# In the opening, TensorE sums the squares tile by tile and multiplies the first modulation tiles

## The chip, the cores and the metric

The kernel runs on one core of one Trainium2 chip, as one program with one launch. The metric is the device time in microseconds of one execution; times before are the median of three runs. A core has TensorE (PE; its weight loads are shown apart as PEld), VectorE (DVE), ScalarE (ACT), GpSimd (POOL) and SyncE (SP), each with its own queue in program order, and 16 DMA engines that carry the loads which SP issues.

## The reference, cut to what matters

Two transformer layers on 512 tokens of 1024 features, all in float32. The changed part is the very beginning of the first layer: the modulation vectors from `c`, the RMS norm of `x`, and the projection `h @ w_in` that reads it.

```python
c_act = jax.nn.silu(c)
for l in range(DEPTH):
    mod = c_act @ w_ada[l] + b_ada[l]
    sh1, sc1, g1, sh2, sc2, g2 = [t[:, None, :] for t in jnp.split(mod, N_ADA, axis=-1)]
    h = rmsnorm(x, norm_mix_g[l]) * (1.0 + sc1) + sh1
    z = h @ w_in[l]
    ...                                   # four attention mixers, then the gated output and the MLP
```

`rmsnorm` divides `x` by the root of the mean of its squares over the 1024 features and multiplies by a gain.

## The kernel before

Activations lie transposed: `x` is eight tiles `X["x"][k]` of 128 features by 512 tokens. A float32 product is made of three fp32r products: a weight tile is split into `whi` (ACT, line 87) and `wlo` (the rest, here on POOL in two halves, line 91), an activation tile into `hhi` and `hlo`, and PE multiplies hi by hi, hi by lo and lo by hi. `Weights` keeps the queue of weight tiles: `_load` issues the load into one of four raw buffers (line 72), `_split` makes hi and lo, and `get` runs ahead by `load_ahead` and `split_ahead`.

`start` is the opening. SP loads `x` (lines 165, 168), then two weight tiles, then the rest in the order of the code. PE first spreads the silu of `c` over all partitions (`cbP`, 8 products with the identity). ACT squares the eight tiles of `x`, DVE adds them up into `sqacc`, and PE turns the sum into four columns `nsum` with four one-column products (`ones` moves, the sum is the weight). DVE scales them (`rsv`, line 253), POOL takes the power -1/2 (`rs`, line 257), PE spreads the result over the partitions (`rsb`, line 263).

Then follows one turn for each tile k: `ada_start` loads two tiles of modulation weights (`ada`, 128 outputs by 1024, line 200), and DVE multiplies each by `cbP` and sums it into a column of `mod` (line 191); ACT makes the gain `gs`; DVE makes `ht = x * gs * rsb`; ACT adds the shift and rounds (`hhi`); ACT adds the shift again, and POOL subtracts for `hlo` (DVE does so from k = 5 on). Five weight tiles are fetched and split in the first turns, as `AHEAD` and `LAHEAD` say. Last come the 120 products `pj`: five weight tiles by eight k by three, with k outside.

A tile scheduler orders each engine's instructions from the order of the code and from marks like `tc.issue_after(last["ada"].ins)`, which put an instruction behind another in that order. An engine works its queue in order, so an instruction that waits holds up all that stand behind it.

Of the kernel before, what the change touches and what calls it, by code (L numbers as in the profile page):

```python
# [10 lines left out]
F32 = mybir.dt.float32  # L11
F32R = mybir.dt.float32r
AF = mybir.ActivationFunctionType
ALU = mybir.AluOpType
# [3 lines left out]
P = 128  # L18
S = 512
D = 1024  # L20
KT = D // P
NADA = 1
AHEAD = (1, 3, 2, 1, 0, 0)
LAHEAD = (2, 3, 2, 1, 0, 0)
PRELOAD = 2
NSPLIT = 3
# [5 lines left out]
NQ = S // P  # L32
# [6 lines left out]
OFF_NMIX, OFF_NMLP, OFF_BADA, OFF_QG, OFF_KVG, OFF_POS, OFF_SINK = 0, 8, 16, 64, 66, 67, 99  # L39
# [8 lines left out]
def wbytes_views(raw, k, n):  # L48
    return raw[:, 0 : k * n].rearrange("p (k n) -> p k n", k=k)


class Weights:
# [23 lines left out]
    def _split(self):  # L76
        i = self.n_split
        while self.n_load <= i:
            self._load()
        ap, k, n, split, rows, pool_lo = self.src[i]  # L80
        raw, flat = self.raws.pop(i)
        if split:
            pool, nb = self.other_pool.get(i, (self.hl_pool, None))
            hi = pool.tile([P, 1024], F32R, tag="whi", name=f"whi{i}", bufs=nb)
            lo = pool.tile([P, 1024], F32R, tag="wlo", name=f"wlo{i}", bufs=nb)
            vh, vl = wbytes_views(hi, k, n), wbytes_views(lo, k, n)
            self.nc.scalar.activation(vh[0:rows], raw[0:rows], AF.Copy)  # L87
            eng = self.nc.gpsimd if pool_lo else self.nc.vector
            for c in ((0, k * n // 2), (k * n // 2, k * n)) if pool_lo else ((0, k * n),):
                c = slice(*c)  # L90
                eng.tensor_tensor(  # L91
                    lo[0:rows, c], flat[0:rows, c], hi[0:rows, c].bitcast(F32), op=ALU.subtract
                )
            self.parts[i] = (vh, vl)
        else:
            self.parts[i] = (raw, None)
        self.n_split += 1
# [12 lines left out]
def layer_stack(ctx: ExitStack, tc: tile.TileContext, a, out):  # L110
    nc = tc.nc
# [5 lines left out]
    wkp = ctx.enter_context(tc.tile_pool(name="wkp", bufs=2))  # L117
    xp = ctx.enter_context(tc.tile_pool(name="xp", bufs=1))
    psA = ctx.enter_context(tc.tile_pool(name="psA", bufs=3, space=PSUM))
    psT = ctx.enter_context(tc.tile_pool(name="psT", bufs=2, space=PSUM))  # L120
# [3 lines left out]
    def mmbank(name):  # L124
        return psA.tile([P, 512], F32, tag="mm", name=name)
# [4 lines left out]
    vecs = cons.tile([P, NV], F32, name="vecs")  # L130
    nc.sync.dma_start(vecs, a["vecs"])
    X = {}
# [4 lines left out]
    ones = cons.tile([P, 1], F32, name="ones")  # L137
# [22 lines left out]
    def load_x(src, queue):  # L160

        v = xp.tile([P, KT // 2, S], F32, tag="V", name="x")
        tiles = [v[:, k, :] for k in range(KT // 2)]
        for k in (0, 2):
            queue.dma_start(v[:, k : k + 2, :], src[:, k : k + 2, :])
        for k in range(KT // 2, KT):
            tiles.append(xp.tile([P, S], F32, tag="KL", name="x", bufs=4))
            queue.dma_start(tiles[k], src[:, k, :])
        X["x"] = tiles


    cact = cons.tile([P, KT], F32, name="cact")
# [10 lines left out]
    mod = [cons.tile([P, 6, KT], F32, name=f"mod{l}") for l in range(DEPTH)]  # L183

    W = Weights(nc, rawp, hlp, 3, 3)
# [10 lines left out]
    def ada_start(pool, m, cv):  # L196

        raw = pool.tile([P, 2, 1024], F32, tag="ada0", name="ada0", bufs=4)
        for part in (1, 0):
            nc.sync.dma_start(raw[:, part, :], a["wadaP"][m, :, part, :])  # L200
            ada_cols(raw[:, part, :], 0, part, m, cv)
# [4 lines left out]
    last = {}  # L206
# [941 lines left out]
    def start(pool, n):  # L1148


        nonlocal psS
        load_x(a["xT"], nc.sync)
        for _ in range(PRELOAD):
            W._load()
        cps = ctx.enter_context(ExitStack())
        psC = cps.enter_context(tc.tile_pool(name="psC", bufs=1, space=PSUM))
        cbP = psC.tile([P, D], F32, name="cbP")
        for k in range(KT):
            nc.tensor.matmul(
                cbP[:, k * P : (k + 1) * P], cact[:, k : k + 1].to_broadcast([P, P]), ident,  # L1160
                start=True, stop=True,
            )
        acc = wkp.tile([P, S], F32, tag="sqacc", name="sqacc", bufs=1)
        nc.scalar.activation(acc, X["x"][0], AF.Square)
        for k in range(1, KT):
            sq = mmbank("sq")
            nc.scalar.activation(sq, X["x"][k], AF.Square)
            nc.vector.tensor_tensor(acc, acc, sq, op=ALU.add)
        rsb = psO.tile([P, 512], F32, tag="po", name="rsb0")
        ps = psT.tile([P, 512], F32, tag="pt", name="nsum")  # L1170
        for j in range(NQ):
            nc.tensor.matmul(
                ps[:, j : j + 1], acc[:, j * P : (j + 1) * P], ones, start=True, stop=True
            )
        r = rstd_cols(ps, NQ, [(0, NQ, 1.0 / D)])
        bcast_cols(rsb, r, 0, NQ)
        hs = h_tiles(hsp, "hs", 16)
        pss = [mmbank("pj") for _ in range(min(n, 3))]
        pss += [psT.tile([P, 512], F32, tag="pt", name="pj") for _ in range(min(n, 5) - 3)]
        W.other_pool.update({i: (pool, 4) for i in range(4)})  # L1180
        ws = []
        gs = smp.tile([P, KT], F32, tag="gs", name="gs")
        for k in range(KT):
            ada_start(pool, k, cbP)
            if k < n:
                W.split_ahead, W.load_ahead = AHEAD[k], LAHEAD[k]
                with tc.issue_after(last["pow"].ins):
                    ws.append(W.get())
            g = vecs[:, OFF_NMIX + k : OFF_NMIX + k + 1]
            nc.scalar.activation(  # L1190
                gs[:, k : k + 1], mod[0][:, 1, k : k + 1], AF.Identity, bias=g, scale=g
            )
            t = tmp_tile("ht")
            hi, lo = hs[k]
            with tc.issue_after(last["ada"].ins):
                last["dve"] = nc.vector.scalar_tensor_tensor(
                    t, X["x"][k], gs[:, k : k + 1], rsb, op0=ALU.mult, op1=ALU.mult
                )
            nc.scalar.activation(hi, t, AF.Identity, bias=mod[0][:, 0, k : k + 1])
            if k < KPOOL:  # L1200
                nc.scalar.activation(t, t, AF.Identity, bias=mod[0][:, 0, k : k + 1])
                nc.gpsimd.tensor_tensor(lo, t, hi.bitcast(F32), op=ALU.subtract)
            else:
                last["dve"] = nc.vector.scalar_tensor_tensor(
                    lo, t, mod[0][:, 0, k : k + 1], hi.bitcast(F32), op0=ALU.add, op1=ALU.subtract
                )
        for _ in range(NADA):
            i = ada_state["i"]
            raw = pool.tile([P, 2, 1024], F32, tag="ada0", name="ada0", bufs=4)
            nc.sync.dma_start(raw, a["wadaD"][i : i + 2].rearrange("t p r -> p t r"))  # L1210
            with tc.issue_after(last["dve"].ins):
                for j in range(2):
                    ada_cols(raw[:, j, :], *ada_todo[i + j], cbP)
            ada_state["i"] += 2
        W.split_ahead, W.load_ahead = 3, 3
        while W.n_split < n + NSPLIT:
            W._split()
        load_consts()
        nc.scalar.activation(cb, cbP, AF.Copy)
        cps.close()  # L1220
        psS = ctx.enter_context(tc.tile_pool(name="psS", bufs=2, space=PSUM))
        def part(g, w, k, h):
            nc.tensor.matmul(
                pss[g], ws[g][w][:, k, :], hs[k][h], start=(k + w + h == 0),
                stop=(k == KT - 1 and w == 1),
            )


        for k in range(KT - 1):
            for w, j, h in ((0, k, 0), (0, k - 1, 1), (1, k - 2, 0)):  # L1230
                if j >= 0:
                    for g in range(n):
                        part(g, w, j, h)
        k = KT - 1
        for g in range(n):
            for w, j, h in (
                (0, k - 1, 1), (1, k - 2, 0), (1, k - 1, 0), (0, k, 0), (0, k, 1), (1, k, 0)
            ):
                part(g, w, j, h)
        return hs, pss  # L1240
# [74 lines left out]
def _layout(i):  # L1315
    f = np.float32
    i = {k: np.asarray(v) for k, v in i.items()}
    a = _shape_constants()
# [6 lines left out]
    for l in range(DEPTH):  # L1325
        b = l * VL
# [13 lines left out]

    wa = i["w_ada"].transpose(0, 2, 1).reshape(DEPTH, 6, KT, P, D)
    a["wadaP"] = wa[0, 0:2].transpose(1, 2, 0, 3)
    a["wadaD"] = np.concatenate(
        [wa[0, j] for j in (2, 4, 3, 5)] + [wa[1, j] for j in (1, 0, 2, 4, 3, 5)]
    )
# [47 lines left out]
```

## Time and profile before

| | us |
|---|---|
| median of 3 runs | 1293.07 (1290.05 to 1298.04) |
| the profiled execution | 1297.35 |
| its span | 1295.4 |
| PE busy | 1242.8 (96%) |
| PE weight loads busy | 1046.6 (81%) |
| DVE busy | 691.1 (53%) |
| ACT busy | 592.1 (46%) |
| POOL busy | 541.3 (42%) |
| mean granted clock of PE | 0.98 |

Durations below come from the profiled execution, whose own time lies 4.3 us over the median. Busy shares are means over the whole span; in the first 32 us PE has 17.5 us of work, in most later stretches nearly all.

### The profile page before, as it was taken

To read this page: it belongs to the slowest core of one execution; us is meant where nothing else is said; L and a number is where in the kernel's file an instruction comes from. 1 tells how busy PE (TensorE), PEld (TensorE's weight loads), DVE (VectorE), ACT (ScalarE), POOL (GpSimd) and SP (SyncE) were. 2 spreads that over 40 slices of the span, in tenths; PEclk is the share of its full clock that TensorE was granted. 3 is DMA by queue.
4 is the path that set the end of the run, shared out by engine and by line. 5 is a ranking of instruction groups with operands and counts; after the bars stand their busy time and mean duration, and the time that the engine had idled before them with its cause. 6 is when DMAs were issued, how large, how long until landed. Compare 5 with 4: busy or idle time off the path is not lost. (4 is left out here: it accounts for less than half of the span.)

```text
span 1295.4 us, 18013 instructions
## 1 busy us (share of the span) xinstructions
PE 1242.8 (96%) x6572; PEld 1046.6 (81%) x6572; DVE 691.1 (53%) x1562; ACT 592.1 (46%) x1161; POOL 541.3 (42%) x463
## 2 busy tenths in 40 slices
PE   5989999988999999999999999999999999999997
PEld 4878787778888888888898777878988888888887
DVE  5758867966455454554254686786543213123124
ACT  5567768743532232231235766787353223233120
POOL 5423323242645545545425323323364444444440
PEclk7989999998999999999998999999999999999998
DMA  9744324353356766665434412122233323233312
GB/s 341 253 109 159 100 80 147 131 176 117 115 167 207 241 195 217 226 193 195 138 112 120 138 49 66 51 89 78 95 114 97 92 95 94 95 98 98 98 33 66
DMA packets 53129, 171.07 MB, mean 132 GB/s; under 512 B 6065, under 2 KB 9777, under 8 KB 53041
## 3 DMA queue, kind: packets, MB, share of 16 engines
q1 hardware_dynamic: 51312, 165.73, 40.0%
q10 hardware_dynamic: 1728, 4.20, 1.0%
q8 instruction: 52, 0.85, 0.3%
q14 instruction: 37, 0.30, 0.1%
HBM read 163.35 MB, written 4.19 MB: 129 GB/s over the span
## 5 line engine op out<-in xcount | busy, mean ns | idle before, releaser
L91 POOL TENSOR_TENSOR wlo<-raw,whi 128x512 fp32r<-128x512 f32 (+3 forms) x372 | 487.0, 1333 | 549.9 <-ACT whi L87 516.0
L87 ACT ACTIVATE whi<-raw 128x1024 fp32r<-128x1024 f32 (+3 forms) x186 | 193.8, 1046 | 452.8 <-PE px L368 244.5
L369 PE MATMUL pj<-hhi,wlo 128*128 128x512 f32 (+1 forms) x768 | 286.2, 373 | 0.0
L368 PE MATMUL pj<-hlo,whi 128*128 128x512 f32 (+1 forms) x768 | 285.7, 373 | 0.0
L367 PE MATMUL pj<-hhi,whi 128*128 128x512 f32 (+1 forms) x768 | 285.7, 374 | 0.0
L367 PE MATMUL px<-a,whi 128*128 128x512 f32 (+2 forms) x584 | 215.2, 368 | 0.0
L369 PE MATMUL px<-a,wlo 128*128 128x512 f32 (+2 forms) x584 | 214.5, 367 | 0.0
L368 PE MATMUL px<-a,whi 128*128 128x512 f32 (+2 forms) x584 | 213.7, 366 | 0.0
L411 DVE SCALAR_TENSOR_TENSOR x<-px,mod,x 128x512 f32<-128x512 f32 (+2 forms) x95 | 62.7, 665 | 195.1 <-PE px L369 195.0
L368 PEld LDWEIGHTS pj<-hlo,whi 128*128 128x128 f32 x768 | 144.9, 189 | 24.8
L369 PEld LDWEIGHTS pj<-hhi,wlo 128*128 128x128 f32 x768 | 144.9, 189 | 24.4
L367 PEld LDWEIGHTS pj<-hhi,whi 128*128 128x128 f32 x768 | 144.3, 189 | 22.9
L191 DVE CUSTOM_DVE_ANT_0 adaw<-cb,adaw,vecs 128x1024 f32<-128x1024 f32 x78 | 102.6, 1316 | 56.0 <-DMA adaw<-in_wadaD 54.0
L369 PEld LDWEIGHTS px<-a,wlo 128*128 128x128 f32 x584 | 109.8, 188 | 19.2
L368 PEld LDWEIGHTS px<-a,whi 128*128 128x128 f32 x584 | 109.8, 188 | 18.8
L367 PEld LDWEIGHTS px<-a,whi 128*128 128x128 f32 x584 | 109.9, 188 | 17.9
L1134 DVE SCALAR_TENSOR_TENSOR t<-pj,r 128x512 f32<-128x512 f32 x64 | 44.1, 692 | 141.4 <-ACT r L1133 141.2
L449 DVE TENSOR_TENSOR a<-t,a 128x512 fp32r<-128x512 f32 x64 | 82.8, 1296 | 41.8 <-ACT a L448 41.8
L592 ACT ACTIVATE e<-e,nm 128x256 f32<-128x256 f32 (+3 forms) x160 | 85.9, 538 | 10.1 <-DVE nm L587 9.8
L449 DVE TENSOR_TENSOR pl<-pt,ph 128x512 fp32r<-128x512 f32 (+1 forms) x112 | 65.5, 598 | 4.6 <-ACT ph L448 3.7
L626 PE MATMUL pt<-ident,e 128*128 128x128 f32 x376 | 61.0, 278 | 5.4 <-POOL e L570 4.9
L448 ACT ACTIVATE ph<-pt 128x512 fp32r<-128x512 f32 (+1 forms) x112 | 56.1, 524 | 17.7 <-PE pt L626 16.9
(236 smaller groups left out, 1829.9 us busy)
## 6 DMA issues: line engine op xcount, KB each, us to landing
adaw<-in_wadaD SPq DMA_DIRECT2D x78, 512.0 KB, 4.4
raw<-in_wup SPq DMA_DIRECT2D x64, 512.0 KB, 3.5
raw<-in_wdown SPq DMA_DIRECT2D x64, 512.0 KB, 3.6
raw<-in_winT SPq DMA_DIRECT2D x28, 512.0 KB, 3.7
ada<-in_wadaP SPq DMA_DIRECT2D x16, 512.0 KB, 8.9
raw<-in_wout SPq DMA_DIRECT2D x16, 512.0 KB, 3.6
cw<-in_cw SPq DMA_DIRECT2D x4, 512.0 KB, 5.1
raw<-in_cw SPq DMA_DIRECT2D x4, 512.0 KB, 4.6
```

The costliest lines, as they stand in the source:

```text
L87: self.nc.scalar.activation(vh[0:rows], raw[0:rows], AF.Copy)
L91: eng.tensor_tensor(lo[0:rows, c], flat[0:rows, c], hi[0:rows, c].bitcast(F32), op=ALU.subtract)
L191: last["ada"] = nc.vector.tensor_tensor_reduce(out=w, in0=cv, in1=w, scale=1.0, scalar=vecs[:, off : off + 1], op0=ALU.mult, op1=ALU.add, ...
L367: nc.tensor.matmul(ps, wh[:, k, :], hh[:, c], start=first, stop=False)
L368: nc.tensor.matmul(ps, wh[:, k, :], hl[:, c], start=False, stop=False)
L369: nc.tensor.matmul(ps, wl[:, k, :], hh[:, c], start=False, stop=last)
L411: last["dve"] = nc.vector.scalar_tensor_tensor(X["x"][m][:, c], ps, mod[l][:, part, m : m + 1], X["x"][m][:, c], op0=ALU.mult, op1=ALU.add)
L448: nc.scalar.activation(hi, src, AF.Copy)
L449: last["dve"] = nc.vector.tensor_tensor(lo, src, hi.bitcast(F32), op=ALU.subtract)
L592: nc.scalar.activation(e, e, AF.Exp, bias=nm[:, n : n + 1], scale=-1.0, accum_out=den[:, n : n + 1])
L626: nc.tensor.transpose(pt[:, c : c + P], p[n][:, col : col + P], ident)
L1134: nc.vector.scalar_tensor_tensor(t, ps, 0.0, r, op0=ALU.max, op1=ALU.mult)
```

## The change

The sums of squares are no longer added up on DVE. Each squared tile lies in SBUF (`tmp_tile`, four buffers) and PE multiplies it by `ones` at once, four one-column products a tile, summed in PSUM. The modulation tiles of k = 0 come in another layout (`wadaK`: 128 inputs by 8 by 128 outputs), are loaded right after `x` and ahead of the first two weights, and PE multiplies them by `cact` instead of DVE by `cbP`: eight one-column products for each of the two, the gain's (part 1) first, with ACT adding the bias into `mod`. DVE's `ada_start` begins with k = 1. The first split of a weight stands later (`AHEAD[0]` is 0), the first `hhi` is put behind the first `whi`, and one more split is asked for right after it.

```diff
--- before.py
+++ after.py
@@ -20,7 +20,7 @@
 D = 1024
 KT = D // P
 NADA = 1
-AHEAD = (1, 3, 2, 1, 0, 0)
+AHEAD = (0, 3, 2, 1, 0, 0)
 LAHEAD = (2, 3, 2, 1, 0, 0)
 PRELOAD = 2
 NSPLIT = 3
@@ -84,7 +84,7 @@
             hi = pool.tile([P, 1024], F32R, tag="whi", name=f"whi{i}", bufs=nb)
             lo = pool.tile([P, 1024], F32R, tag="wlo", name=f"wlo{i}", bufs=nb)
             vh, vl = wbytes_views(hi, k, n), wbytes_views(lo, k, n)
-            self.nc.scalar.activation(vh[0:rows], raw[0:rows], AF.Copy)
+            self.whi = self.nc.scalar.activation(vh[0:rows], raw[0:rows], AF.Copy)
             eng = self.nc.gpsimd if pool_lo else self.nc.vector
             for c in ((0, k * n // 2), (k * n // 2, k * n)) if pool_lo else ((0, k * n),):
                 c = slice(*c)
@@ -1150,6 +1150,9 @@
 
         nonlocal psS
         load_x(a["xT"], nc.sync)
+        first = pool.tile([P, 2, KT, P], F32, tag="ada0", name="ada0", bufs=4)
+        for part in (1, 0):
+            nc.sync.dma_start(first[:, part], a["wadaK"][part])
         for _ in range(PRELOAD):
             W._load()
         cps = ctx.enter_context(ExitStack())
@@ -1160,17 +1163,27 @@
                 cbP[:, k * P : (k + 1) * P], cact[:, k : k + 1].to_broadcast([P, P]), ident,
                 start=True, stop=True,
             )
-        acc = wkp.tile([P, S], F32, tag="sqacc", name="sqacc", bufs=1)
-        nc.scalar.activation(acc, X["x"][0], AF.Square)
-        for k in range(1, KT):
-            sq = mmbank("sq")
-            nc.scalar.activation(sq, X["x"][k], AF.Square)
-            nc.vector.tensor_tensor(acc, acc, sq, op=ALU.add)
         rsb = psO.tile([P, 512], F32, tag="po", name="rsb0")
         ps = psT.tile([P, 512], F32, tag="pt", name="nsum")
-        for j in range(NQ):
-            nc.tensor.matmul(
-                ps[:, j : j + 1], acc[:, j * P : (j + 1) * P], ones, start=True, stop=True
+        for k in range(KT):
+            sq = tmp_tile("sq")
+            nc.scalar.activation(sq, X["x"][k], AF.Square)
+            for j in range(NQ):
+                nc.tensor.matmul(
+                    ps[:, j : j + 1], sq[:, j * P : (j + 1) * P], ones,
+                    start=(k + j == 0), stop=(k == KT - 1 and j == NQ - 1),
+                )
+
+        aps = psT.tile([P, 512], F32, tag="pt", name="adap")
+        for part in (1, 0):
+            for k in range(KT):
+                nc.tensor.matmul(
+                    aps[:, part : part + 1], first[:, part, k, :], cact[:, k : k + 1],
+                    start=(k == 0), stop=(k == KT - 1),
+                )
+            b = OFF_BADA + 8 * part
+            nc.scalar.activation(
+                mod[0][:, part, 0:1], aps[:, part : part + 1], AF.Identity, bias=vecs[:, b : b + 1]
             )
         r = rstd_cols(ps, NQ, [(0, NQ, 1.0 / D)])
         bcast_cols(rsb, r, 0, NQ)
@@ -1181,7 +1194,8 @@
         ws = []
         gs = smp.tile([P, KT], F32, tag="gs", name="gs")
         for k in range(KT):
-            ada_start(pool, k, cbP)
+            if k:
+                ada_start(pool, k, cbP)
             if k < n:
                 W.split_ahead, W.load_ahead = AHEAD[k], LAHEAD[k]
                 with tc.issue_after(last["pow"].ins):
@@ -1192,12 +1206,16 @@
             )
             t = tmp_tile("ht")
             hi, lo = hs[k]
-            with tc.issue_after(last["ada"].ins):
+            with tc.issue_after(last["ada" if k else "pow"].ins):
                 last["dve"] = nc.vector.scalar_tensor_tensor(
                     t, X["x"][k], gs[:, k : k + 1], rsb, op0=ALU.mult, op1=ALU.mult
                 )
-            nc.scalar.activation(hi, t, AF.Identity, bias=mod[0][:, 0, k : k + 1])
+            with tc.issue_after(W.whi.ins if k == 0 else last["dve"].ins):
+                nc.scalar.activation(hi, t, AF.Identity, bias=mod[0][:, 0, k : k + 1])
+            if k == 0:
+                W._split()
             if k < KPOOL:
+              with tc.issue_after(W.whi.ins if k == 0 else last["dve"].ins):
                 nc.scalar.activation(t, t, AF.Identity, bias=mod[0][:, 0, k : k + 1])
                 nc.gpsimd.tensor_tensor(lo, t, hi.bitcast(F32), op=ALU.subtract)
             else:
@@ -1340,6 +1358,7 @@
 
     wa = i["w_ada"].transpose(0, 2, 1).reshape(DEPTH, 6, KT, P, D)
     a["wadaP"] = wa[0, 0:2].transpose(1, 2, 0, 3)
+    a["wadaK"] = np.stack([i["w_ada"][0][:, D * j : D * j + P].reshape(KT, P, P).transpose(1, 0, 2) for j in (0, 1)])
     a["wadaD"] = np.concatenate(
         [wa[0, j] for j in (2, 4, 3, 5)] + [wa[1, j] for j in (1, 0, 2, 4, 3, 5)]
     )
```

How the instructions stand on PE, from the start of the program to the first two `pj`, before (`cbP` is the spread of `c`, `rsb` that of the norm):

```order
L1159 MATMUL cbP<-ident,cact 128x128 x8
L1172 MATMUL nsum<-ones,sqacc 128x1 x4
L263 MATMUL rsb_170<-ident,rs 128x128 x4
L1223 MATMUL pj<-hhi,whi_213 128x512
L1223 MATMUL pj<-hhi,whi_218 128x512
```

and after:

```order
L1162 MATMUL cbP<-ident,cact 128x128 x8
L1172 MATMUL nsum<-ones,sq 128x1 x32
L1180 MATMUL adap<-cact,ada_131 128x1 x8
L263 MATMUL rsb_150<-ident,rs 128x128 x4
L1180 MATMUL adap<-cact,ada_131 128x1 x8
L1241 MATMUL pj<-hhi,whi_251 128x512
L1241 MATMUL pj<-hhi,whi_260 128x512
```

There are 28 more products of `nsum` and 16 of `adap` ahead of the first `pj`, and the spread of the norm stands between the two groups of `adap`.

On ACT, from the squares to the third weight's `whi`, before (`whi_213` and `whi_218` are the first two weights):

```order
L1164 ACTIVATE sqacc<-x 128x512
L1167 ACTIVATE sq<-x 128x512 x7
L87 ACTIVATE whi_213<-raw_131 128x1024
L87 ACTIVATE whi_218<-raw_133 128x1024
L1190 ACTIVATE gs<-mod_112,vecs 128x1
L87 ACTIVATE whi_238<-raw_211 128x1024
L1199 ACTIVATE hhi<-ht,mod_112 128x512
```

and after (`whi_251`, `whi_260` and `whi_276` are the first three):

```order
L1170 ACTIVATE sq<-x 128x512 x8
L1185 ACTIVATE mod_112<-adap,vecs 128x1
L1204 ACTIVATE gs<-mod_112,vecs 128x1
L1185 ACTIVATE mod_112<-adap,vecs 128x1
L87 ACTIVATE whi_251<-raw_134 128x1024
L1214 ACTIVATE hhi<-ht,mod_112 128x512
L87 ACTIVATE whi_260<-raw_136 128x1024
L1219 ACTIVATE ht<-ht,mod_112 128x512
L87 ACTIVATE whi_276<-raw_249 128x1024
```

The splits of the first two weights stood right behind the squares; now the two copies of the modulation sums and the gain stand ahead of the first, and the first tile's `hhi` between it and the second.

## Rows read from the trace of the kernel before

**Rows 1.** Stretches: us, busy time of PE, PEld, DVE, ACT, POOL, clock, DMA share.
```profile
30.00:35.00 5.00, 5.00 (x23) 4.00 (x23) 5.00 (x9) 2.35 (x6) 2.99 (x3) 1.00 1.02 398
35.00:40.00 5.00, 5.00 (x23) 4.05 (x22) 5.00 (x9) 2.68 (x5) 1.30 (x1) 1.00 1.01 407
```

**Rows 2.** Timeline of PE, opening: start us, us, engine, line, operation, tiles, idle before.
```profile
3.70 3.66 PE L1159 MATMUL cbP<-ident,cact 128*128 128x128 f32 x16 [3.70 <-DVE cact L178]
...
15.62 2.07 PE L263 MATMUL rsb<-ident,rs 128*128 128x128 f32 x8 [1.42 <-POOL rs L257]
...
22.16 2.69 PE L1223 MATMUL pj<-hhi,whi 128*128 128x512 f32 x5 [1.15 <-ACT whi L87]
...
29.48 1.43 PE L1223 MATMUL pj<-hhi,whi 128*128 128x512 f32 x5 [1.51 <-ACT hhi L1199]
30.75 1.33 PE L1223 MATMUL pj<-hlo,whi 128*128 128x512 f32 x5
...
54.07 0.28 PE L554 MATMUL pn<-whi,hhi 128*128 128x268 f32 x1
```

**Rows 3.** Timeline of the weight loads (PEld), opening and layer two.
```profile
12.33 1.78 PEld L1172 LDWEIGHTS nsum<-ones,sqacc 128*128 128x128 f32 x8 [5.17 <-issue]
...
686.38 0.30 PEld L756 LDWEIGHTS mlas<-ones,csq 128*128 128x128 f32 x2
...
688.61 0.30 PEld L759 LDWEIGHTS mlas<-ones,kvq 128*128 128x128 f32 x2
```

**Rows 4.** Stretches with the granted clock (third number from the end).
```profile
7.20:10.40 3.20, 0.15 (x2) 0.00 (x0) 2.78 (x5) 2.37 (x5) 0.00 (x0) 1.00 0.99 372
...
10.00:11.00 1.00, 0.00 (x0) 0.00 (x0) 0.90 (x2) 0.89 (x2) 0.00 (x0) 0.75 1.01 412
...
10.60:27.50 16.90, 10.88 (x30) 7.95 (x31) 10.13 (x17) 9.67 (x14) 12.95 (x11) 0.50 0.98 369
...
686.30:689.70 3.40, 3.40 (x32) 3.40 (x31) 1.81 (x4) 2.12 (x3) 3.35 (x4) 1.00 0.71 182
689.80:691.40 1.60, 1.60 (x9) 1.48 (x7) 1.54 (x3) 0.63 (x1) 0.78 (x2) 0.50 0.83 282
```

**Rows 5.** Timeline of POOL, opening.
```profile
15.53 7.43 POOL L91 TENSOR_TENSOR wlo<-raw,whi 128x512 fp32r<-128x512 f32 x6
22.91 1.31 POOL L1202 TENSOR_TENSOR hlo<-ht,hhi 128x512 fp32r<-128x512 f32 x1
24.16 5.01 POOL L91 TENSOR_TENSOR wlo<-raw,whi 128x512 fp32r<-128x512 f32 x4
29.11 2.57 POOL L1202 TENSOR_TENSOR hlo<-ht,hhi 128x512 fp32r<-128x512 f32 x2
```

**Rows 6.** Timeline of ACT, opening.
```profile
10.06 1.26 ACT L1167 ACTIVATE sq<-x 128x512 f32<-128x512 f32 x2 [0.37 <-DMA x<-in_xT]
11.92 1.06 ACT L87 ACTIVATE whi<-raw 128x1024 fp32r<-128x1024 f32 x1 [0.60 <-DMA raw<-in_winT]
13.18 1.06 ACT L87 ACTIVATE whi<-raw 128x1024 fp32r<-128x1024 f32 x1 [0.21 <-DMA raw<-in_winT]
15.81 0.39 ACT L1190 ACTIVATE gs<-mod,vecs 128x1 f32<-128x1 f32 x1 [1.57 <-DVE mod L191]
```

**Rows 7.** Timeline of DVE, opening.
```profile
14.23 0.16 DVE L253 TENSOR_SCALAR rsv<-nsum 128x4 f32<-128x4 f32 x1 [2.02 <-PE nsum L1172]
14.48 1.28 DVE L191 CUSTOM_DVE_ANT_0 ada<-cbP,ada,vecs 128x1024 f32<-128x1024 f32 x1
...
25.43 1.29 DVE L191 CUSTOM_DVE_ANT_0 ada<-cbP,ada,vecs 128x1024 f32<-128x1024 f32 x1 [3.67 <-DMA ada<-in_wadaP]
```

**Rows 8.** Timeline of SP's issues: the fourth and the fifth weight.
```profile
10.65 7.74 SPq L72 DMA_DIRECT2D raw<-in_winT  x2
```

**Rows 9.** Loads by issue, windows 18.0 to 18.4 and 52.8 to 53.25: size, us to landing.
```profile
raw<-in_winT SPq DMA_DIRECT2D x1, 512.0 KB, 6.1
...
cw<-in_cw SPq DMA_DIRECT2D x1, 512.0 KB, 4.1
```

## What it was predicted to do

> **What bounds the kernel now.** I read the table of stretches first, then the timelines of the engines in the opening, because the change touches only the first 30 us. In the stretches of 5 us TensorE (PE) is busy for all of its time from 30 us on [rows 1]: from there the opening projection runs without a hole, and whatever delays its first dense piece delays everything behind it. PE's timeline [rows 2] shows where that piece begins: the products of feature tile 2 (the tiles are counted from 0) start at 29.48, the five with `hlo` of tile 1 follow at 30.75, and the next stage begins at 54.07. Of the 120 products 15 (five weights by `hhi` 0, `hhi` 1 and `hlo` 0) are done before 29.48; the other 105 take 24.6 us, 0.234 each. Before 29.48 PE mostly waits. So the question is when `hhi` 2 and `hlo` 1 are ready, and what they wait for.
>
> `hlo` of tile 1 is made by GpSimd (POOL). POOL's timeline [rows 5] has no hole from 15.53 on: ten half weights `wlo` and two `hlo`, done at 29.11 + 2.57 = 31.7 with a third `hlo` (that of tile 2), so the second `hlo` was done at 30.4, a mere 0.35 before PE took it. This chain of 14.9 us starts when POOL may begin with `wlo` of the first weight, and is a bound almost as tight as the one PE shows. `hhi` of tile 2 waited for a modulation tile that landed at 25.43 [rows 7]; that load stands in SP's queue behind the fifth weight, whose issue waited until 18.1 for a raw buffer, free only after the first weight's `wlo` [rows 8]. Both therefore hang on the first weight's split.
>
> **What it removes.** Seven additions on DVE go and eight squares on ACT stay. The additions trail the squares, so they hide nothing else and DVE has no other work there. Two modulation tiles no longer go through DVE, 1.28 us each [rows 7]; DVE waits soon after for a landing, so this is worth nothing on the path either.
>
> **What it adds on PE.** The four one-column products of the sums become 32, the two modulation tiles another 16. In all: 32 + 8 + 4 (`rsb`) + 8 = 52 products of fp32, in the profile two instructions each, so 64 + 16 + 8 + 16 = 104, one behind the other between `cbP` and the first `pj`. They are weight loads in the main: 128x128 is loaded for one column. Two prices stand in the trace. In the opening eight loads of `nsum` took 1.78 us, 0.2225 each, at a granted clock of 0.50 (1.2 GHz) [rows 3, 4]. In layer two the same shape (`mlas`) advanced from 686.38 to 688.61 in 20 loads, 0.1115 each, at a granted clock of 1.00 (2.4 GHz) [rows 3, 4].
>
> Which price holds depends on the clock. After `cbP` the granted clock was 1.00 from about 7.2, PE idled, and it fell to 0.50 at about 10.5 (the stretch 10 to 11 has 0.75) and stayed there to 27.5 [rows 4]. In the new kernel PE doesn't idle there. But the trace has the very case: at 686.3 to 689.7 PE was busy for 3.40 of 3.40 us, mostly with one-column products, and from 689.8 the granted clock was 0.50 [rows 4]. I take this as the nearest row, since idling and a run of one-column products were both followed by the lower level: 1.00 from 7.2 to 10.5, 0.50 after.
>
> The sum on PE: `cbP` is through at about 7.2. To 10.5 there is time for 3.3 / 0.1115 = 30 instructions; the squares come fast enough for that (the last two are done at 11.3 [rows 6]). The other 74 take 74 x 0.2225 = 16.5 us: `nsum` ends at 18.1 instead of 14.1, the first modulation tile at 21.6, `rsb` at 23.4, the second modulation tile at 27.0. The power on POOL fits in between: from `rsv` to `rsb` it was 14.23 to 15.62 [rows 2, 7], so it is ready at 19.6, under the first modulation tile.
>
> **What that moves on ACT and POOL.** ACT takes its instructions in order, and in the new order the copy of the second modulation sum stands ahead of the first weight's `whi`. The weight lands early (at the third place of the loads, 14.5, where DVE's first tile landed [rows 7]), but lies there: the copy (0.1 and 0.39, as `gs` [rows 6]) ends at 27.5, `whi` (1.06 [rows 6]) at 28.5. So POOL begins its chain at 28.6 and not at 15.53: 13.0 us later. The same twelve instructions, 14.9 us, end at 43.5. POOL waits for nothing else in them: the fifth weight is issued after the first `wlo` (28.6 + 2.5 = 31.1), lands 4.1 to 6.1 us later (a load on an empty queue, and the same load before [rows 9]) at 35.2 to 37.2, and its turn on POOL comes at 39.9.
>
> **What is late next.** The tile that held up `hhi` of tile 2 lands one slot (13.18 - 11.92 = 1.26 [rows 6]) behind the fifth weight, at 36.5 to 38.5; from there to PE's use it took 29.48 - 25.43 = 4.05 [rows 2, 7], so 40.5 to 42.5, under POOL's 43.5. PE therefore resumes its dense run at 43.5 where before it stood at 30.75: 12.8 us later. Those behind it (constants, the next weights, the copy of `cb`) move with it, since they are queued behind the same instructions; I find nothing later that is timed from elsewhere. `hhi` of tile 2 is late by 11.0 to 13.0, so what is queued on DVE and ACT may stand up to 12.8 - 11.0 = 1.8 better towards PE than before: a give-back between 0 and 1.8, of which I take 0, as PE's own queue is the later one.
>
> Two terms have bounds of their own. If the rise of the clock at 7.2 doesn't come in another execution, 30 instructions cost 30 x 0.111 = 3.3 us more; the one profile shows it, so I take 0. When PE resumes, the clock may still be at 0.50: before, it was so to 27.5 though PE had work with few holes from 22.16 [rows 2, 4]; half speed over these 5.4 us costs up to 2.7. PE has some fifteen products to do just before 43.5, as it had before 29.48, so I take 0 here too. Together: +12.8, from +11.0 to +18.8.
>
> The Trainium skill, "TensorE: Matmul & The Clock Gate", section "Why this matters for your kernels", says to keep TensorE busy without a break to have its higher clock. By that, the 52 products would hold the clock themselves; the stretch at 686.3, busy throughout and followed by 0.50, speaks against it. The same page's section "LDWEIGHTS (loading the stationary operand)" gives a load about 107 ns for 128 columns, whatever the clock; by that estimate the 104 would end at 18.3 and the gain or loss be that of the first rival below. The trace's 0.2225 at the lower clock is twice that.
>
> **Rival 1: the clock stays full.** If the granted clock stays at 1.00 through the 104 instructions, they take 104 x 0.1115 = 11.6 us: `nsum` ends at 14.3, as early as now, the second modulation tile at 18.8, `whi` at 20.4, POOL's chain at 35.3. PE resumes 4.5 us late: 1293.07 + 4.5 = 1297.6. For it: PE has no hole. Against it: row 686.3. I give it 0.12.
>
> **Rival 2: the added products are as cheap as one column.** The place is the run of `nsum` behind the squares. If a group of four took less than the 0.6 us of a square (0.075 an instruction), PE would keep pace with the loads: sums at 11.6, modulation tiles at their landings (11.9 and 13.2, where the weights landed [rows 6]), the first weight at 14.5, `whi` at 15.5, POOL at 15.6 against 15.53, and the time is 1293, not slower. Only 0.2225 and 0.1115 are measured, both above 0.075, for the same shape; 0.05.
>
> **How the numbers follow.** The profiled execution took 1297.35 (span 1295.4), 4.3 more than the median of the three runs, 1293.07, which lie between 1290.05 and 1298.04. Against itself the sum is 1297.35 + 12.8 = 1310.2; against the median 1305.9, which I predict. The forecast has 0.80, with a range of its own of 1304.1 to 1311.9; the rivals have 0.12 and 0.05, and 0.03 is left for what I don't see. The range reaches from rival 1 to the upper bound: 1297 to 1312. A difference within 1% (12.9 us, up to 1306.0) is about what a measurement of this kernel can't tell from no change. The forecast stands just on that line: the terms above it (clock) and below it (give-back) share its 0.80 about evenly, 0.42 over it and 0.38 under. With both rivals under the line: slower 0.43, same 0.54, faster 0.03.
>
> **What would show it.** In the changed kernel's profile: `nsum` in 64 PE instructions, 0.11 each up to some 10.5 and 0.22 after, ending near 18; the granted clock 0.50 through the modulation products; the first `whi` at about 27.5 to 28.5, with ACT waiting for PE `adap` ahead of it; POOL from about 28.6; a hole on PE before `hlo` of tile 1 at about 43.5; the next stage (`pn`) at about 66.9 instead of 54.07. I am wrong if the clock is 1.00 between 10.5 and 20, if a one-column product costs under 0.1 us an instruction, if `whi` doesn't wait for the modulation copy, or if the 12.8 us are there at 67 us and gone by the end.

## The result, and the profile after

The changed kernel takes 1309.69 us, the median of four runs (1304.37 to 1312.04); beside them the kernel before took 1293.04 (1290.05 to 1298.04). The ratio is 1.0109, 95% interval 1.0083 to 1.0136: about 14 us slower by the ratio (the medians lie 16.7 apart), close to the 12.9 us that the prediction took as the line between no change and slower. The forecast was 1305.9, range 1297 to 1312. The profiled execution took 1311.79, span 1310.0.

All of the loss arises before the opening projection runs at its full pace. First TensorE's weight loads, in the timeline of the changed kernel (columns as in [rows 2]):

```profile
3.70 3.49 PEld L1162 LDWEIGHTS cbP<-ident,cact 128*128 128x128 f32 x16 [3.70 <-DVE cact L178]
7.06 13.77 PEld L1172 LDWEIGHTS nsum<-ones,sq 128*128 128x128 f32 x64
20.72 3.53 PEld L1180 LDWEIGHTS adap<-cact,ada 128*128 128x128 f32 x16
24.13 1.83 PEld L263 LDWEIGHTS rsb<-ident,rs 128*128 128x128 f32 x8
25.84 3.53 PEld L1180 LDWEIGHTS adap<-cact,ada 128*128 128x128 f32 x16
```

There is no hole from 3.70 to 29.4. The 64 loads of the sums take 13.77 / 64 = 0.215 us each, close to the 0.2225 that the prediction took from [rows 3, 4] for the lower clock, from the first to the last; they end at 20.84, where the eight of before ended at 14.11. Who waits for that, on ACT, DVE and POOL, and in SP's issues (one fence for each):

```profile
9.07 0.63 ACT L1170 ACTIVATE sq<-x 128x512 f32<-128x512 f32 x1 [0.88 <-PE nsum L1172]
...
24.37 0.26 ACT L1185 ACTIVATE mod<-adap,vecs 128x1 f32<-128x1 f32 x1 [9.56 <-PE adap L1180]
...
29.49 0.26 ACT L1185 ACTIVATE mod<-adap,vecs 128x1 f32<-128x1 f32 x1 [4.44 <-PE adap L1180]
29.65 1.05 ACT L87 ACTIVATE whi<-raw 128x1024 fp32r<-128x1024 f32 x1
...
42.45 0.72 ACT L1214 ACTIVATE hhi<-ht,mod 128x512 fp32r<-128x512 f32 x1 [1.57 <-DVE ht L1210]
```

```profile
20.96 0.16 DVE L253 TENSOR_SCALAR rsv<-nsum 128x4 f32<-128x4 f32 x1 [17.32 <-PE nsum L1172]
```

```profile
21.27 1.02 POOL L257 TENSOR_TENSOR rs<-rsv,mhalf 128x4 f32<-128x4 f32 x1 [20.28 <-DVE rsv L253]
30.78 4.97 POOL L91 TENSOR_TENSOR wlo<-raw,whi 128x512 fp32r<-128x512 f32 x4 [8.48 <-ACT whi L87]
35.70 1.28 POOL L1220 TENSOR_TENSOR hlo<-ht,hhi 128x512 fp32r<-128x512 f32 x1
36.94 7.47 POOL L91 TENSOR_TENSOR wlo<-raw,whi 128x512 fp32r<-128x512 f32 x6
44.37 2.53 POOL L1220 TENSOR_TENSOR hlo<-ht,hhi 128x512 fp32r<-128x512 f32 x2
```

```profile
9.94 23.69 SPq L72 DMA_DIRECT2D raw<-in_winT  x2
```

Read from the top: ACT runs out of `tmp_tile` buffers at the fifth square, then waits 9.56 and 4.44 us for the modulation sums. Right behind the second copy comes the first `whi`, and POOL, idle for 8.48 us after the power, starts its halves at 30.78 instead of 15.53 [rows 5]. The second `hlo` is done at 45.65. SP holds the fifth weight until 33.3. PE's timeline and its stretch show the end of it:

```profile
43.22 1.44 PE L1241 MATMUL pj<-hhi,whi 128*128 128x512 f32 x5 [1.01 <-ACT hhi L1214]
45.70 2.35 PE L1241 MATMUL pj<-hlo,whi 128*128 128x512 f32 x5 [1.05 <-POOL hlo L1220]
47.85 1.99 PE L1241 MATMUL pj<-hhi,wlo 128*128 128x512 f32 x5
49.68 1.33 PE L1241 MATMUL pj<-hhi,whi 128*128 128x512 f32 x5
...
70.59 0.28 PE L554 MATMUL pn<-whi,hhi 128*128 128x268 f32 x1
```

```profile
45.00:50.00 5.00, 4.29 (x12) 3.43 (x13) 5.00 (x9) 3.05 (x5) 3.19 (x3) 0.66 1.03 412
50.00:55.00 5.00, 5.00 (x23) 4.05 (x22) 5.00 (x9) 1.51 (x4) 1.31 (x1) 1.00 1.02 407
```

PE resumes at 45.70, 14.95 us later than at 30.75 [rows 2]; its first two groups of five, 2.15 and 1.83 us from start to start instead of 1.17, run mostly at the lower clock (0.66 in 45 to 50; the granted clock falls at 45.9 and is back at 49.3); `pn` is 16.5 us late. With the DVE instructions of both kernels laid side by side the lateness is 15.2 us at 104 us and 14.6 at the end: some 2 us are given back, most of them in the first mixers, and the rest stays.

### The profile page after: what moved, and what is told of

It reads as the page before. It is cut to its first block, busy times and chain, and to the rows that moved or that the text cites. A ratio compares the mean times of both kernels' runs of the same rounds, so it can differ in the third digit from the quotient of the medians.

```text
span 1310.0 us, 18178 instructions
## 1 busy us (share of the span) xinstructions
PE 1263.7 (96%) x6660; PEld 1066.6 (81%) x6660; DVE 683.3 (52%) x1551; ACT 592.6 (45%) x1163; POOL 542.7 (41%) x463
## 5 line engine op out<-in xcount | busy, mean ns | idle before, releaser
L449 DVE TENSOR_TENSOR a<-t,a 128x512 fp32r<-128x512 f32 x64 | 82.2, 1287 | 41.8 <-ACT a L448 41.8
L448 ACT ACTIVATE ph<-pt 128x512 fp32r<-128x512 f32 (+1 forms) x112 | 56.2, 524 | 16.2 <-PE pt L626 15.2
```

Source lines behind the costliest of these rows:

```text
L448: nc.scalar.activation(hi, src, AF.Copy)
L449: last["dve"] = nc.vector.tensor_tensor(lo, src, hi.bitcast(F32), op=ALU.subtract)
```

## The experiments

Four theories were open. **A**, the prediction's: PE's added one-column products delay the modulation sums, ACT's order puts the first `whi` behind them, and POOL's chain of 14.9 us then sets the end. **B**: one half of the change alone, or ACT's order alone, makes the loss. **C**: it is the late loads; the fifth weight's raw buffer waits for the first `wlo`, and `hhi` of tile 2 stands behind. **D**: a one-column product costs 0.215 in the opening whatever the clock, so the clock has no part in it. The times of each group of runs stand against the kernel before on the same chip: 1294.63 (1290.45 to 1299.71, 21 runs) for the first four, 1295.84 (1290.75 to 1298.5, 14 runs) for the next four. The numbers in this table are from the timelines (us; start of the first `wlo`, end of `hlo` 1, start of `pn`) and from the timed runs:

| kernel | `nsum` ends | first `wlo` | `hlo` 1 ends | `pn` | median (range, runs) | ratio, 95% interval |
|---|---|---|---|---|---|---|
| before | 14.11 | 15.53 | 30.42 | 54.07 | | |
| after | 20.84 | 30.78 | 45.65 | 70.59 | 1309.69 (1304.37 to 1312.04, 4) | 1.0109, 1.0083 to 1.0136 |
| c_after | 17.78 | 27.72 | 42.59 | 66.70 | 1308.05 (1305.82 to 1310.51, 4) | 1.011, 1.0077 to 1.0142 |
| e1_split_first | 17.92 | 19.34 | 37.88 | 61.27 | 1304.14 (1296.94 to 1309.18, 10) | 1.0067, 1.0043 to 1.0091 |
| e2_mod_only | 14.68 | 24.20 | 39.09 | 64.01 | 1302.47 (1300.81 to 1303.9, 6) | 1.0063, 1.0042 to 1.0083 |
| e3_sums_only | 20.84 | 22.26 | 37.14 | 60.51 | 1300.48 (1298.32 to 1303.03, 10) | 1.0042, 1.0022 to 1.0062 |
| e4_raw5 | 17.89 | 27.83 | 42.72 | 68.58 | 1312.36 (1311.0 to 1314.19, 4) | 1.0128, 1.0108 to 1.0148 |
| e6_dense | 21.35 | 22.77 | 38.92 | 62.39 | 1305.54 (1301.99 to 1309.53, 5) | 1.0079, 1.0051 to 1.0108 |
| e8_split_mod | 14.81 | 16.27 | 34.76 | 58.24 | 1298.24 (1295.24 to 1300.82, 10) | 1.0026, 1.001 to 1.0042 |

**The changed kernel again** (c_after), no edit.

> The changed kernel once more, as the standard for the runs beside it and as another sample of the clock at the start. My theory: one-column products cost what their weight load costs, 0.215 us an instruction at the lower clock, and the 104 of them set when the second modulation sum, the first whi and POOL's chain come. In this sample the sums end at 20.8 (no rise of the clock after the spread of c) or near 18.1 (with it), POOL's first wlo starts at 30.8 or near 28, and the time is 12 to 17 us over the kernel before. Rival theories expect the same time, from other causes.

The same ratio, 1.011. Its profile differs from the first in the clock: in the price of the sums, and in the level at which PE does `hhi` 2. Its weight loads, its stretches, and ACT and PE:

```profile
6.93 10.85 PEld L1172 LDWEIGHTS nsum<-ones,sq 128*128 128x128 f32 x64
17.66 3.53 PEld L1180 LDWEIGHTS adap<-cact,ada 128*128 128x128 f32 x16
```

```profile
10.20:17.70 7.50, 7.50 (x37) 7.50 (x37) 0.00 (x0) 0.92 (x2) 0.00 (x0) 0.50 1.03 415
17.70:26.30 8.60, 8.60 (x41) 8.60 (x41) 3.17 (x5) 0.65 (x2) 1.02 (x1) 0.50 0.20 78
26.30:44.20 17.90, 12.49 (x25) 7.25 (x26) 8.91 (x16) 11.57 (x18) 16.23 (x14) 0.50 0.70 265
```

```profile
26.43 0.26 ACT L1185 ACTIVATE mod<-adap,vecs 128x1 f32<-128x1 f32 x1 [4.44 <-PE adap L1180]
26.59 1.05 ACT L87 ACTIVATE whi<-raw 128x1024 fp32r<-128x1024 f32 x1
```

```profile
40.24 2.50 PE L1241 MATMUL pj<-hhi,whi 128*128 128x512 f32 x5 [0.98 <-ACT hhi L1214]
42.65 2.15 PE L1241 MATMUL pj<-hlo,whi 128*128 128x512 f32 x5
...
66.70 0.28 PE L554 MATMUL pn<-whi,hhi 128*128 128x268 f32 x1
```

Here the granted clock was at 1.00 behind `cbP`, as before [rows 4], and fell at 10.1 though PE had no hole; behind the fall it was busy for 7.50 of 7.50 us. The clock stayed at 0.50 until 44.3. That is the prediction's clock case, and `pn` at 66.70 is near its 66.9. One of its signs is missing in this profile: there is no hole on PE before `hlo` 1, because the five products of `hhi` 2, at the lower clock, last until 42.65, and `hlo` 1 is done at 42.59. In the first profile the clock didn't rise behind `cbP`: the sums took 2.9 us more.

**The splits ahead of the modulation copies** (e1), on the changed kernel:

```diff
+        W.other_pool.update({i: (pool, 4) for i in range(4)})
+        for _ in range(2):
+            W._split()
         aps = psT.tile([P, 512], F32, tag="pt", name="adap")
...
-            nc.scalar.activation(
+            with tc.issue_after(W.whi.ins):
+                nc.scalar.activation(
```

> The changed kernel with the first two weights split on ACT ahead of the copies of the modulation sums. My theory: POOL's chain is freed from ACT and starts behind the power, at about 22.3 (8.5 us earlier), but the sums still end at 20.8 and hhi 0 still waits for the second modulation sum at 29.7; hlo 1 comes at about 39.8 instead of 45.6, so 4 to 8 us faster than the changed kernel, and still 7 to 11 us slower than the kernel before. Rival (ACT's order alone is the cost, the products are cheap cover): all of it comes back, within 2 us of the kernel before. Rival (the late fifth load): its issue moves from 33.3 to about 25, so 8 us come back as well, but then with hhi 2, not hlo 1, as the last to be ready.

By the ratios 1.011 became 1.0067, some 5.6 us less than the changed kernel and 8.7 more than the kernel before (its runs scatter widely, from 1296.94 to 1309.18): ACT's order is a part of the loss, and not the whole of it. POOL shows where the rest sits:

```profile
19.34 4.94 POOL L91 TENSOR_TENSOR wlo<-raw,whi 128x512 fp32r<-128x512 f32 x4
27.86 2.51 POOL L91 TENSOR_TENSOR wlo<-raw,whi 128x512 fp32r<-128x512 f32 x2 [3.58 <-ACT whi L87]
```

The first two weights are split at once, but the third `whi` stands behind the second modulation copy on ACT (26.7), and POOL waits 3.58 us for it.

**Modulation alone** (e2: the changed kernel with `sqacc` on DVE as before) and **sums alone** (e3: the kernel before with the changed loop for `nsum`). Short, as the two code blocks of the change's diff are exchanged:

```diff
# e2, on the changed kernel
-        for k in range(KT):
-            sq = tmp_tile("sq")
...
+        acc = wkp.tile([P, S], F32, tag="sqacc", name="sqacc", bufs=1)
...
# e3, on the kernel before
-        acc = wkp.tile([P, S], F32, tag="sqacc", name="sqacc", bufs=1)
...
+        for k in range(KT):
+            sq = tmp_tile("sq")
...
```

> Only the modulation tiles on TensorE; the sums of squares on VectorE as in the kernel before. My theory: 56 of the 88 added instructions' worth of sums go, the four sum products end at 14.1, the second modulation sum at about 22.4, first whi ends at 24, POOL starts at 24.0 (before 15.5, changed 30.8): 7 to 10 us slower than before. Rival (order alone): as the changed kernel, 13 to 16 us slower, since ACT's order is the same. Rival (sums alone are the cost): within 2 us of before.

> Only the sums of squares on TensorE; the modulation tiles of k = 0 on VectorE, loads and ACT's order as in the kernel before. My theory: the sums end at 20.8 (or 18.1 if the clock rises after the spread of c), POOL is behind the power and starts at 22.4 (19.6): 4 to 8 us slower than before. The lateness of POOL in this run and in the run with the modulation alone should add up to the 15.2 us of the changed kernel. Rival (order alone): the order of before is restored, so within 2 us of before. Rival (modulation alone is the cost): within 2 us of before.

Each costs a part, 1.0063 and 1.0042, together 1.05% against 1.1% for both. POOL's start says the same, without what the clock does later: 24.20 and 22.26 against 15.53 are 8.7 and 6.7 us, together 15.4; the whole change has 15.25 in the first profile, in which, as in e3, all the sums ran at the lower clock. Their first rows on POOL, e2 and then e3:

```profile
24.20 4.96 POOL L91 TENSOR_TENSOR wlo<-raw,whi 128x512 fp32r<-128x512 f32 x4 [8.06 <-ACT whi L87]
```

```profile
22.26 7.44 POOL L91 TENSOR_TENSOR wlo<-raw,whi 128x512 fp32r<-128x512 f32 x6
```

In e2 POOL waits for ACT's `whi`; in e3 there is no wait, since the power itself comes that late. Theory B falls.

**The fifth weight loaded early** (e4), on the changed kernel:

```diff
-        raw = self.raw_pool.tile([P, 1024], F32, tag="raw", name=f"raw{i}")
+        if i == 4:
+            raw = self.hl_pool.tile([P, 1024], F32, tag="whi", name=f"raw{i}")
+        else:
+            raw = self.raw_pool.tile([P, 1024], F32, tag="raw", name=f"raw{i}")
```

> The changed kernel, with the raw tile of the fifth weight taken from the pool of the halves, so that its load no longer waits for the first weight's wlo on POOL. Theory (POOL's chain of wlo and hlo, which starts behind the first whi, sets the end of the opening): the fifth weight lands before 20 instead of 34 to 37, and nothing else moves: hlo of tile 1 is ready within 1.5 us of where it was against the start of that chain (14.9 us behind the first wlo), and the time is that of the changed kernel, 1306 to 1311, about 1.1% over the kernel before. Rival (the late load of the fifth weight, and of the modulation tile behind it in SP's queue, holds up hhi 2 and with it the opening): pn comes some 8 us earlier than in the changed kernel, at about 59 to 62, and the time falls by 6 to 8 us, to 0.5% over the kernel before.

The fifth weight is issued at 11.1 instead of 30 to 33, `hhi` 2 ends at 36.1 instead of 40.2 (c_after), and nothing is gained: 1.0128. POOL in e4, PE, and the stretch in which PE resumes:

```profile
34.01 7.47 POOL L94 TENSOR_TENSOR wlo<-raw,whi 128x512 fp32r<-128x512 f32 x6
41.45 5.04 POOL L1223 TENSOR_TENSOR hlo<-ht,hhi 128x512 fp32r<-128x512 f32 x4
```

```profile
37.72 1.45 PE L1244 MATMUL pj<-hhi,whi 128*128 128x512 f32 x5
42.78 2.50 PE L1244 MATMUL pj<-hlo,whi 128*128 128x512 f32 x5 [3.61 <-POOL hlo L1223]
```

```profile
42.00:48.00 6.00, 5.22 (x12) 4.13 (x13) 6.00 (x9) 2.33 (x5) 4.48 (x4) 0.50 1.00 370
```

PE now does `hhi` 2 at 37.72 and then waits 3.61 us for POOL, which is where it was. Theory C falls: in the changed kernel the two come at nearly the same time (waits of 1.01 and 1.05), but POOL alone is enough to hold PE. `pn` comes 1.9 us later than in c_after, at 68.58, though `hlo` 1 is done at the same time: the clock fell at 41.4, in PE's wait, and was at 0.50 until 48.2.

**Denser products among the sums** (e6), on the changed kernel: 64 PE instructions more, of the same values.

```diff
-        for k in range(KT):
+        for k in [*range(KT)] * 2:
             nc.tensor.matmul(
                 cbP[:, k * P : (k + 1) * P], cact[:, k : k + 1].to_broadcast([P, P]), ident,
...
                     start=(k + j == 0), stop=(k == KT - 1 and j == NQ - 1),
                 )
+            for _ in range(3):
+                nc.tensor.matmul(
+                    cbP[:, k * P : (k + 1) * P], cact[:, k : k + 1].to_broadcast([P, P]), ident,
+                    start=True, stop=True,
+                )
```

> The changed kernel, with the spread of c done twice and, behind the four products of each squared tile, three of the spread's products repeated (128 columns each, the same values), so 64 PE instructions more in the same stretch; the result is not changed. Theory (the price of a one-column product follows the clock, and the clock falls because one-column products alone don't hold it): with the denser products among them the clock is 1.00 in the sums, a load of nsum takes about 0.11 us, and the last one ends at about 21 to 23 in spite of the added work. Rival A (a one-column product costs 0.215 in the opening whatever the clock is): nsum ends at 33 to 38. Rival B (the clock falls for the sums with or without the added products): a clock of 0.50 in the records between 11 and 25, and the end of nsum again at 30 or later. The whole time by the theory: within 3 us of the changed kernel; by the rivals 10 to 15 us more.

Its weight loads (the pair of rows at 9.44 and 10.33 comes eight times), and its stretches:

```profile
9.44 0.97 PEld L1172 LDWEIGHTS nsum<-ones,sq 128*128 128x128 f32 x8
10.33 0.75 PEld L1177 LDWEIGHTS cbP<-ident,cact 128*128 128x128 f32 x6
11.00 0.97 PEld L1172 LDWEIGHTS nsum<-ones,sq 128*128 128x128 f32 x8
```

```profile
9.40:21.40 12.00, 12.00 (x110) 12.00 (x110) 0.00 (x0) 4.41 (x6) 0.00 (x0) 1.00 0.86 346
21.90:25.30 3.40, 3.40 (x33) 3.40 (x33) 0.31 (x1) 0.65 (x2) 3.40 (x4) 1.00 0.01 2
25.40:27.50 2.10, 2.10 (x11) 2.10 (x10) 2.10 (x4) 0.00 (x0) 2.10 (x2) 0.50 0.52 109
```

The clock is 1.00 all through the sums, fourteen instructions take 1.56 us (11.00 - 9.44), 0.111 each, and the last sum ends at 21.35 in spite of the added work. Theory D falls, and rival B of the expectation with it. PE stays without a hole, and yet at 25.4, in the second half of the modulation products, the clock is at 0.50 again. The whole time is no test of this: ACT's order in this kernel came out with the first two `whi` ahead of the modulation copies, as in e1. That is the likely reason why it is 7 us under e4 where I expected 3 at most; no run separates the two. Against e1's 1.0067 its 1.0079 shows no gain from the clock: with the added work the sums end 3.4 us later than in e1.

**Modulation alone, with the splits first** (e8): e2 and e1 in one.

> The modulation tiles on TensorE as in the changed kernel, but the sums of squares on DVE as before, and the first two weights' splits asked for ahead of the copies of the modulation sums on ACT. Theory (of the cost of the modulation on TensorE, most is that ACT's first whi and with it POOL's chain stand behind the copy of the second sum): POOL starts its wlo at about 16 instead of 24, the copy ends at about 23, hlo of tile 1 is ready at 33 to 34, and the kernel is 2 to 4 us slower than before (0.2 to 0.3%). Rival (the modulation products on PE, or the later gain and shift, hold the opening in themselves): hlo of tile 1 at 37 or later, and 6 to 8 us slower, as with the copy ahead (0.5 to 0.65%).

The ratio is 1.0026, 3.4 us over before (2.4 between the medians), where e2 was at 1.0063; `pn` is 4.2 us late where e2 had 9.9. So of what the modulation on PE costs, some three fifths is the place of the copy on ACT. POOL's rows show the rest, again the third `whi` behind the second copy:

```profile
16.27 4.95 POOL L91 TENSOR_TENSOR wlo<-raw,whi 128x512 fp32r<-128x512 f32 x4
24.75 2.51 POOL L91 TENSOR_TENSOR wlo<-raw,whi 128x512 fp32r<-128x512 f32 x2 [3.53 <-ACT whi L87]
```

`hlo` 1 came at 34.76, a little later than the 33 to 34 that I had expected.

**The theory used on the kernel before** (e7, run once, and e9, the same kernel, nine runs): the raw tile as in e4 (not shown again), and the first half weights ahead of the power on POOL.

```diff
...
-        r = rstd_cols(ps, NQ, [(0, NQ, 1.0 / D)])
+        W.other_pool.update({i: (pool, 4) for i in range(4)})
+        W._split()
+        with tc.issue_after(W.first.ins):
+            r = rstd_cols(ps, NQ, [(0, NQ, 1.0 / D)])
...
```

> The kernel before, with the raw tile of the fifth weight from the pool of the halves and the first weight's wlo ahead of the power on POOL, so that POOL's chain starts earlier. Theory (POOL's chain sets the end of the opening in the kernel before as well): wlo starts at about 13 to 14 instead of 15.5, and pn at 52.5 to 53.5 instead of 54.07; a gain of about 1 us, too small for the times to show. Rival (POOL's chain isn't what holds the opening before): pn within 0.3 us of 54.07 or later.

> The kernel before with the fifth weight's raw tile from the pool of the halves and the first wlo ahead of the power on POOL, the same as the single look at it (pn at 52.45 against 54.07, a span 1.3 us shorter), now timed. Theory (what POOL's chain gains in the opening stays to the end): 1 to 2 us less than the kernel before, a ratio of 0.9985 to 0.9992, which the interval may just not tell from 1. Rival (given back in the later stages): a ratio of 1.000 or more, with pn again at about 52.5.

e7 had `pn` at 52.45 and took 1296.06, once. e9: 1290.95 (1287.9 to 1294.39, 9 runs) against 1296.47 (1291.8 to 1299.27, 14 runs), a ratio of 0.9962, 95% interval 0.9945 to 0.9978: some 4.9 us faster than the kernel before, where I expected 1 to 2. POOL and PE in e9:

```profile
12.60 2.50 POOL L95 TENSOR_TENSOR wlo<-raw,whi 128x512 fp32r<-128x512 f32 x2 [11.60 <-ACT whi L91]
...
27.18 2.57 POOL L1209 TENSOR_TENSOR hlo<-ht,hhi 128x512 fp32r<-128x512 f32 x2
```

```profile
27.38 1.44 PE L1230 MATMUL pj<-hhi,whi 128*128 128x512 f32 x5
28.65 1.33 PE L1230 MATMUL pj<-hlo,whi 128*128 128x512 f32 x5
...
51.87 0.28 PE L559 MATMUL pn<-whi,hhi 128*128 128x268 f32 x1
```

POOL begins 2.9 us earlier, PE takes `hlo` 1 2.1 earlier and reaches `pn` 2.2 earlier. Two things came earlier here, and no run tries them apart: `hhi` 2, for which PE waited before (29.48 [rows 2], now 27.38), and `hlo` 1 (done at 30.42, now at 28.5). The early raw tile alone could not have brought more than some 0.3 of the 2.1, since POOL's chain before had no hole and ended at 30.42, 0.33 ahead of PE's 30.75; that is argued from the rows, not run. So POOL's chain is, within 0.3 us, a bound of the opening of the kernel before, too. The gain, 2.9 to 7.1 us by the interval, is over the 2.2 of the opening; what the rest is stays open.

One distance holds through all these kernels and bears theory A out: from the end of `hlo` 1, which lies anywhere from 28.5 to 45.65 us, to the start of `pn` it is 23.4 to 23.7 us in seven of the eleven profiles. In the other four (after, c_after, e2, e4) it is 24.1 to 25.9, and there PE's first five products with `hlo` 1 took 1.98 to 2.29 us from start to start, at the lower clock, instead of 1.17 to 1.27.

## Why the prediction was right

The path was the forecast's, step by step; what differs is the clock, whose two bounded terms I had both taken at 0.

- **The sums on PE.** 64 loads, done at 18.1 by the forecast. With the rise of the clock after `cbP` they ended at 17.78, 17.92 and 17.89 (c_after, e1, e4), without it at 20.84 (after, e3): the term "if the rise doesn't come, 3.3 more" was real and measured 3.0, in two of five profiles. One profile of before had shown the rise, and I took one case for the rule.
- **Modulation, ACT, POOL's start.** The second copy done at 27.5 and POOL at 28.6 in the forecast; 26.69 and 27.72 in c_after, 29.75 and 30.78 in the first profile. Of the 0.9 that c_after is early, 0.3 is the sums; 0.4 is the load, (24.13 - 20.72) / 16 = 0.213 from start to start where I had divided a group's length, 1.78 / 8, with the tail of its last load in it, forty times; the rest is in the copy and `whi`.
- **POOL's chain.** 14.9 us as read from [rows 5]; measured 14.87 in both profiles (45.65 - 30.78, 42.59 - 27.72). This was the strongest term; e4 and the distance from `hlo` 1 to `pn` show that it is the bound.
- **The clock when PE resumes.** Taken at 0, bound 2.7. The two low groups cost 2.15 + 1.83 - 2 x 1.17 = 1.6 us in the first profile; in c_after one group took 1.98 for 1.17, 0.8. I had argued that PE's work before the resume would be as before; but there the clock had come up at 27.6, three us before PE resumed at 30.75, and stayed up. Here it fell again at 45.9, just behind the resume, until 49.3 in the first profile, and rose only at 44.3, behind the resume, in c_after.
- **Give-back.** Taken at 0, bound 1.8, expected on DVE's and ACT's queues; some 2 us came back in the mixers instead. What gave them back in the first profile stays open: the changed kernel is there at 0.50 for as long in sum (76.6 to 80.0 and 100.5 to 103.9) as the kernel before (82.2 to 89.0). In c_after, too, the lateness fell, from 12.6 at `pn` to 10.7 at 104 us, and was 12.8 again at 230, where it is at 0.50 twice as long as the kernel before (235.4 to 242.2 against 225.5 to 229.0). That this is the clock's doing fits, but no run tests it.
- **The sum.** 12.8 forecast; in the first profile 12.8 + 2.2 (PE's resume at 45.70 for 43.5) + 1.5 = 16.5 at `pn`, and 14.6 at the end; in c_after 12.6 at `pn` and 13.3 at the end. That c_after meets the forecast so closely at `pn` is in part luck: POOL's start 0.9 early and the clock's 0.8 nearly cancel. The timed ratio gives 1.0109 x 1293.07 = 1307.2, 1.3 over the forecast, and the median itself is 3.8 over: two terms that can only add had each been left at 0.

**Rival 1**, the clock stays full, fell: 0.50 for 7.50 us of unbroken work in c_after. The rule to keep PE busy, which the Trainium skill gives ("TensorE: Matmul & The Clock Gate", section "Why this matters for your kernels"), isn't borne out by these products: PE was busy and the clock fell. In e6, with 128-column products among them, it stayed at 1.00 through the 12.00 us of the sums. **Rival 2**, products cheaper than 0.075 an instruction, fell: an instruction took 0.215 or 0.111 in all profiles. On the same page of the Trainium skill, the section "LDWEIGHTS (loading the stationary operand)" has one figure for the load, about 107 ns for 128 columns; the runs have 0.111 at the full clock and 0.215 at half of it.

## What to carry to other kernels

In these runs a reduction by one-column products cost its weight loads at the clock that held, 0.111 or 0.215 us each. So count the loads, and take the price at the lower clock too: busy as PE was with them, the clock fell under them here. When work moves to an idle engine, look at what stands behind its result in another engine's queue: on ACT the copy of 0.26 us, waiting for the products, held up the splits and with them POOL's chain. And look at a chain on a slow engine that ends just before its user needs it: the kernel before got faster when POOL's chain, 0.3 us ahead of PE, began earlier and the late load was issued earlier with it.

## What the runs showed of the hardware

The rise of the clock in the opening isn't sure: the same kernel, with the same `cbP` ahead, was at 1.00 from 6.7 on in one execution (c_after) and had no rise before the sums' end in another (after). In the latter the column of the clock prints 1.00 for the stretches up to 42, where the trace has no clock record (its first is at 42.5); the duration of a load, 0.215, is what tells the level there.

Executions of one kernel also part later. e7 and e9 are the same program; laid against the kernel before they are 3.6 us ahead, both, at 205 us, and at the end 1.3 and 5.8. One of the two places where they part is a pause of PE in layer two, here in the stretches of e7 and then of e9:

```profile
686.00:690.00 4.00, 4.00 (x29) 3.75 (x28) 2.19 (x4) 1.73 (x4) 3.06 (x3) 0.82 0.75 224
690.00:694.00 4.00, 2.93 (x14) 2.87 (x14) 1.65 (x5) 1.22 (x3) 2.02 (x4) 0.50 0.43 156
```

```profile
686.00:690.00 4.00, 3.56 (x21) 3.24 (x21) 2.52 (x6) 1.82 (x3) 2.70 (x5) 0.66 0.66 217
690.00:694.00 4.00, 4.00 (x35) 4.00 (x34) 2.33 (x4) 1.20 (x3) 1.08 (x1) 1.00 0.43 98
```

e7 runs the second of these stretches at 0.50, e9 at 1.00, and PE does 14 and 35 products in it; e9's low clock lies in the first (0.66) and is over sooner, at 688.7 against 695.4. e1 parts further: its profiled execution, the fastest of its ten, is 7.2 us late at `pn` and 0.3 ahead of the profile of before at the end, while its timed runs are 8.7 over. So the end of one profiled execution can miss an effect in the opening by more than 7 us; a place shortly behind the change, as `pn` here, tells it closely, and the timed runs tell the whole.
